# Update of x, squares and normalised tokens in two pieces of 512 columns at the stage boundaries of a four-layer network

## The chip, the cores and the metric

The kernel runs on one core of one Trainium2 chip. The metric is the device time of one launch in microseconds (us), median of the runs. The core has five engines with a queue each: PE (TensorE: matmuls and transposes; its weight loads are listed apart as PEld), DVE (VectorE), ACT (ScalarE), POOL (GpSimd) and SP (SyncE, which issues the loads of weights). An engine takes its queue in order; between engines, semaphores say when a result is there.

## The reference, cut to what matters

```python
def rms_norm(x, g):
    y = x * lax.rsqrt(jnp.mean(x * x, axis=-1, keepdims=True) + RMS_EPS)
    return y * g

def swiglu(x, w_gate, w_up, w_down):
    return (jax.nn.silu(x @ w_gate) * (x @ w_up)) @ w_down

for i in range(DEPTH):                                   # 4 layers
    f = swiglu(rms_norm(x, norm_pre[i, 0]), ...)
    x = x + FFN_HALF * rms_norm(f, norm_post[i, 0])      # FFN_HALF = 0.5
    hn = rms_norm(x, norm_pre[i, 1])
    m = dilated, differential or sliding-window attention of hn, by i % 3
    x = x + rms_norm(m, norm_post[i, 1])
    f = swiglu(rms_norm(x, norm_pre[i, 2]), ...)
    x = x + FFN_HALF * rms_norm(f, norm_post[i, 2])
```

x has 256 tokens of 1024 columns, the FFN 2816 inner columns; everything is fp32.

## The kernel before

**Stages.** Each layer is three stages, an FFN, a mixer (attention) and a second FFN, numbered s = 0 to 11 through the network; s = 1, 4, 7, 10 are the mixers. Between stage s and stage s + 1 lies a boundary; there are eleven. The 256 tokens are two token blocks, t = 0 and t = 1, of 128 tokens each, which lie on the 128 partitions; x stays on the chip as `x[:, t]`, 128 x 1024 for each t.

**Products.** An fp32 product is made of three matmuls of a cheaper type: `mm3` (L173 to L176) multiplies hi by hi, hi by lo and lo by hi, where hi is a rounded copy of an operand and lo what the rounding left off. So each weight unit (128 x 2048, 1 MB) is loaded by SP into a raw buffer (`load_next`, 3 raw buffers), then split (`split_next`): hi is a cast on ACT (L141), lo a subtraction on DVE or, for one unit at each boundary, on POOL (L142). Four units may be split ahead. `pump` takes up the units that are used and starts the next split and load for each.

**A boundary.** `closing` runs the last product of a stage, whose result (`acc`, two banks of 512 columns) is the f or m of the reference. Its last units (four in an FFN) are done for token block 0 first, then `boundary_elem(0)`; then for token block 1, and within the last of these units `norm_tr(0)` is placed; then `boundary_elem(1)`. For one token block, `boundary_elem_` does:

- ACT: Square of the two halves of acc, each with its row sum (L249).
- DVE: u = acc x factor x gain, in two halves (L255).
- POOL: `rstd_of`, the mean (L219) and its power -1/2 (L221).
- DVE: x = u x rstd + x, one instruction of 1024 columns (L259).
- then `norm_elem` for the next stage: ACT Square of x with row sum (L230), POOL mean (L217) and power (L221), DVE hn = x x rstd x gain (L235).

`norm_tr_` then brings hn into the layout of the next stage: PE transposes four blocks of 128 columns into a bank (L281), ACT casts the bank to the hi part of xT (L284), DVE subtracts to get the lo part (L285). This is done twice for each token block: the first L281, L284, L285 for columns 0 to 511, the second for columns 512 to 1023.

**The next stage's start.** An FFN starts with the products g (gate) of token block 0 with two units, then u (up) of token block 0 with two units, then the same for token block 1; `norm_tr(1)` stands in the middle of the last u unit of token block 0. A mixer starts in the same manner with `lead` products. The third matmul of an mm3, L176, takes xT's lo part, which L285 wrote; L174 and L175 take the hi part, which L284 wrote. In the mixer of s = 7 the lead products end with a bias product (L592), whose operand cb is written by ACT and DVE (L450).

**What sets the order.** The Tile framework's scheduler writes each engine's queue when the program is built, from the dependences, priorities (`boundary_elem` runs at a raised priority, PRI = 300; `norm_tr(0)` at PR2 = 8) and its own costs. So an edit may move instructions that it doesn't touch. At the last boundary (s = 11, the end of the program) x is updated in two pieces of 512 columns already (L265), since each is stored at once.

Of the kernel before, what the change touches and what calls it, by code (L numbers as in the profile page):

```python
# [8 lines left out]
F32 = mybir.dt.float32  # L9
F32R = mybir.dt.float32r  # L10
BF16 = mybir.dt.bfloat16
AF = mybir.ActivationFunctionType
ALU = mybir.AluOpType

P = 128
SEQ = 256
D = 1024
# [28 lines left out]
def tile_network(  # L46
# [27 lines left out]
    act, dve, pe, pool = nc.scalar, nc.vector, nc.tensor, nc.gpsimd  # L74
# [4 lines left out]
    small = ctx.enter_context(tc.tile_pool(name="small", bufs=6))  # L79
# [99 lines left out]
    x = actp.tile([P, 2, D], F32, name="x")  # L179
# [31 lines left out]
    def rstd_of(a, b, whole=False):  # L211

        ms = small.tile([P, 1], F32, tag="ms", name="ms")
        if whole:
            pool.tensor_scalar(out=ms, in0=a, scalar1=b, scalar2=None, op0=ALU.add)
        elif b is None:
            pool.tensor_scalar(out=ms, in0=a, scalar1=EPS, scalar2=None, op0=ALU.add)  # L217
        else:
            pool.tensor_scalar(out=ms, in0=a, scalar1=b, scalar2=EPS, op0=ALU.add, op1=ALU.add)  # L219
        r = small.tile([P, 1], F32, tag="rstd", name="rstd")  # L220
        state["rstd"] = pool.tensor_tensor(out=r, in0=ms, in1=half, op=ALU.pow).ins  # L221
        return r
# [2 lines left out]

    def norm_elem(t, s, parts=1):

        ss = small.tile([P, 1], F32, tag="ssx", name="ssx")
        hn = actp.tile([P, D], F32, tag="w", name="hn", bufs=3)
        act.activation(out=hn, in_=x[:, t], func=AF.Square, scale=1.0 / 32.0, accum_out=ss)  # L230
        r = rstd_of(ss, None)
        state["norm"] = state["rstd"]
        for c in range(parts):
            cs = slice(c * D // parts, (c + 1) * D // parts)
            i = dve.scalar_tensor_tensor(out=hn[:, cs], in0=x[:, t, cs], scalar=r, in1=gains["pre", s][:, cs],  # L235
                                     op0=ALU.mult, op1=ALU.mult)
        hn_of[t] = hn, s
        return i

    def boundary_elem(t, s, acc, mid):  # L240
        mid()
        with tc.high_priority(PRI):
            boundary_elem_(t, s, acc)

    def boundary_elem_(t, s, acc):

        ss = small.tile([P, 2], F32, tag="ssf", name="ssf")
        for i in range(2):
            act.activation(out=junk, in_=acc[i], func=AF.Square, scale=1.0 / 32.0,  # L249
                           accum_out=ss[:, i:i + 1])  # L250
        u = actp.tile([P, 2, 512], F32, tag="w", name="u", bufs=3)
        fac = 1.0 if s % 3 == 1 else 0.5
        g = gains["post", s].rearrange("p (i n) -> p i n", i=2)
        for i in range(2):
            dve.scalar_tensor_tensor(out=u[:, i], in0=acc[i], scalar=fac, in1=g[:, i],  # L255
                                     op0=ALU.mult, op1=ALU.mult)
        r = rstd_of(ss[:, 0:1], ss[:, 1:2])
        if s + 1 < 3 * DEPTH:
            dve.scalar_tensor_tensor(out=x[:, t], in0=u.rearrange("p i n -> p (i n)"), scalar=r,  # L259
                                     in1=x[:, t], op0=ALU.mult, op1=ALU.add)  # L260
            norm_elem(t, s + 1)
            return
        for i in range(2):
            cs = slice(i * 512, (i + 1) * 512)
            dve.scalar_tensor_tensor(out=x[:, t, cs], in0=u[:, i], scalar=r, in1=x[:, t, cs],  # L265
                                     op0=ALU.mult, op1=ALU.add)
            nc.sync.dma_start(out=out[:, t, cs], in_=x[:, t, cs])
# [739 lines left out]
    if True:  # L1007
# [10 lines left out]
        with tc.high_priority(PRI):  # L1018
            i = norm_elem(0, 0, 2)
            j = norm_tr(0)  # L1020
# [3 lines left out]
        with tc.issue_after(j.ins):  # L1024
            norm_elem(1, 0)
# [158 lines left out]
```

## Time and profile before

| | us |
|---|---|
| median of 3 runs | 2312.66 (2312.63 to 2313.06) |
| the profiled execution | 2313.26 |
| its span, first to last instruction | 2311.4 |

The mean granted clock of TensorE over the span is 0.998 of full speed. 32467 instructions ran. The core read 401.5 MB from memory, 174 GB/s over the span. Of the chain of work that ended last, 91% is PE's, 3% DVE's, and 2% each POOL's and ACT's.

The span is what the profiler saw of instructions; the profiled execution's own time is 1.9 us more. Busy times are sums over the span, a share of it stands behind each. A timeline row gives an instruction's start and duration, and in brackets how long the engine stood idle before it and which instruction's end released it, where that is known. Matmuls are pipelined, so one begins before its predecessor's end: their pace is read from the starts.

### The profile page before, as it was taken

The numbers are of one execution on the slowest core, as the hardware profiler recorded it, in microseconds if no ns is written. First come the engines' busy times: TensorE is split into PE (matmuls) and PEld (weight loads), VectorE is DVE, ScalarE is ACT, GpSimd is POOL, SyncE is SP. The second block draws the span as 40 slices with busy tenths as digits, with TensorE's granted clock in tenths as the row PEclk, the third lists the DMA queues.
The fourth block names the chain that finished last, engine by engine and source line by source line (L and its number), as shares of the span: only waits on it lengthen the run. The fifth ranks groups of instructions, "written<-read, shape, count | busy, mean of one in ns | idle before, by whom it ended". The sixth has DMA issues, their size and how long they took to land.

```text
span 2311.4 us, 32467 instructions
## 1 busy us (share of the span) xinstructions
PE 2278.0 (99%) x12912; PEld 1999.4 (87%) x12912; DVE 1252.8 (54%) x1830; ACT 1199.0 (52%) x2102; POOL 634.0 (27%) x640
## 2 busy tenths in 40 slices
PE   8999999999999999999999999999999999999998
PEld 6888999988888889788888887788888899998887
DVE  6545544565455555565465558655655544446553
ACT  5435666654444446654354448544444466666442
POOL 0004877620020028620020024100200287773000
PEclk9999999999999999999999999999999999999999
DMA  7554444445545544255555542555555544343552
GB/s 286 185 186 172 171 151 151 155 182 182 182 183 211 183 162 176 92 218 182 185 203 188 187 169 92 191 191 182 190 192 183 190 169 151 140 156 139 216 182 91
DMA packets 60498, 404.65 MB, mean 175 GB/s; under 512 B 6965, under 2 KB 7866, under 8 KB 16314
## 3 DMA queue, kind: packets, MB, share of 16 engines
q1 hardware_dynamic: 60202, 402.51, 47.9%
q8 instruction: 101, 1.65, 0.3%
q14 instruction: 51, 0.42, 0.1%
q10 hardware_dynamic: 144, 0.07, 0.0%
HBM read 401.50 MB, written 1.05 MB: 174 GB/s over the span
## 4 chain that ended last, share of the span: by engine, by line
PE 91%; DVE 3%; POOL 2%; ACT 2%; issue 1%; DMA 1%; SPq 0%; POOLq 0%; DVEq 0%; ACTq 0%
PE gu L175 11%; PE gu L176 11%; PE gu L174 11%; PE acc L176 8%; PE acc L174 8%; PE acc L175 7%; PE qk L175 4%; PE qk L174 4%; PE qk L176 4%; PE v L174 2%; PE v L175 2%; PE v L176 2%; PE tp L373 2%; PE tp L816 2%; POOL lo L142 1%; DVE lo L142 1%
## 5 line engine op out<-in xcount | busy, mean ns | idle before, releaser
L141 ACT CAST hi<-raw 128x1024 fp32r<-128x1024 f32 (+2 forms) x970 | 776.1, 845 | 765.5 <-PE gu L176 322.5
L142 DVE TENSOR_TENSOR lo<-raw,hi 128x1024 fp32r<-128x1024 f32 (+1 forms) x546 | 661.5, 1250 | 549.6 <-ACT hi L141 549.3
L142 POOL TENSOR_TENSOR lo<-raw,hi 128x512 fp32r<-128x512 f32 (+1 forms) x424 | 546.7, 1324 | 147.7 <-ACT hi L141 147.4
L174 PE MATMUL gu<-hi,xT 128*128 128x512 f32 (+1 forms) x1280 | 474.2, 370 | 0.0
L176 PE MATMUL gu<-hi,xT 128*128 128x512 f32 (+1 forms) x1280 | 471.0, 368 | 0.0
L175 PE MATMUL gu<-lo,xT 128*128 128x512 f32 (+1 forms) x1280 | 471.0, 368 | 0.0
L219 POOL TENSOR_SCALAR ms<-ssf 128x1 f32<-128x1 f32 x24 | 7.2, 302 | 1418.9 <-ACT junk L249 1417.9
L176 PE MATMUL acc<-hi,hT 128*128 128x512 f32 x704 | 276.1, 392 | 0.0
L175 PE MATMUL acc<-lo,hT 128*128 128x512 f32 x704 | 275.9, 392 | 0.0
L176 PEld LDWEIGHTS gu<-hi,xT 128*128 128x128 f32 x1280 | 241.3, 188 | 40.0
L174 PE MATMUL acc<-hi,hT 128*128 128x512 f32 x704 | 275.6, 391 | 0.0
L174 PEld LDWEIGHTS gu<-hi,xT 128*128 128x128 f32 x1280 | 241.4, 189 | 39.2
L175 PEld LDWEIGHTS gu<-lo,xT 128*128 128x128 f32 x1280 | 241.4, 189 | 39.1
L174 PE MATMUL qk<-xT,hi 128*128 128x256 f32 x800 | 225.7, 282 | 0.0
L175 PE MATMUL qk<-xT,hi 128*128 128x256 f32 x800 | 222.8, 279 | 0.0
L176 PE MATMUL qk<-xT,lo 128*128 128x256 f32 x800 | 222.7, 278 | 0.0
L176 PEld LDWEIGHTS acc<-hi,hT 128*128 128x128 f32 x704 | 132.2, 188 | 28.4
L175 PEld LDWEIGHTS acc<-lo,hT 128*128 128x128 f32 x704 | 132.2, 188 | 27.8
L174 PEld LDWEIGHTS acc<-hi,hT 128*128 128x128 f32 x704 | 132.3, 188 | 26.2
L174 PEld LDWEIGHTS qk<-xT,hi 128*128 128x128 f32 x800 | 151.3, 189 | 0.2
L176 PEld LDWEIGHTS qk<-xT,lo 128*128 128x128 f32 x800 | 150.6, 188 | 0.1
L175 PEld LDWEIGHTS qk<-xT,hi 128*128 128x128 f32 x800 | 150.3, 188 | 0.2
(265 smaller groups left out, 3364.6 us busy)
## 6 DMA issues: line engine op xcount, KB each, us to landing
raw<-in_w_ffn_dram SPq DMA_DIRECT2D x263, 1024.0 KB, 4.8
raw<-in_w_a_qk_dram SPq DMA_DIRECT2D x48, 1024.0 KB, 4.8
raw<-in_w_a_v_dram SPq DMA_DIRECT2D x32, 768.0 KB, 4.2
raw<-in_w_a_out_dram SPq DMA_DIRECT2D x8, 1024.0 KB, 4.8
raw<-in_w_b_qk_dram SPq DMA_DIRECT2D x8, 1024.0 KB, 4.8
gain<-in_g_pre_dram SPq DMA_DIRECT2D x12, 512.0 KB, 6.1
gain<-in_g_post_dram SPq DMA_DIRECT2D x12, 512.0 KB, 7.2
raw<-in_w_b_v_dram SPq DMA_DIRECT2D x4, 1024.0 KB, 4.8
```

What stands on the lines that cost most here:

```text
L141: act.copy(out=hi[:, cs], in_=r[:, cs])
L142: eng.tensor_tensor(out=lo[:, cs], in0=r[:, cs], in1=hi[:, cs].bitcast(F32), op=ALU.subtract)
L174: pe.matmul(o, lhsT=a[0], rhs=b[0], start=first, stop=False)
L175: pe.matmul(o, lhsT=a[0], rhs=b[1], start=False, stop=False)
L176: pe.matmul(o, lhsT=a[1], rhs=b[0], start=False, stop=last)
L219: pool.tensor_scalar(out=ms, in0=a, scalar1=b, scalar2=EPS, op0=ALU.add, op1=ALU.add)
L373: pe.transpose(tp[:, i * P:(i + 1) * P], h[:, i * P:(i + 1) * P], ident)
L816: pe.transpose(tp[:, c0:c0 + P], src, ident)
```

## The change

For the eleven boundaries, the update of x becomes two instructions of 512 columns, and `norm_elem` is called with two parts: its Square becomes two ACT instructions of 512 columns with a sum each, hn two DVE instructions of 512 columns, and POOL's mean adds the two sums. In the changed file lines stand lower by some: L230 is L232, L235 is L238, L249 is L252, L255 is L258, L259 is L264, L281 is L286, L284 is L289, L285 is L290; L141, L142, L174 to L176 and L217 to L221 stay. At the program's start, `norm_elem(0, 0, 2)` had hn in two parts already; there the Square becomes two as well.

```diff
--- before.py
+++ after.py
@@ -225,10 +225,13 @@
 
     def norm_elem(t, s, parts=1):
 
-        ss = small.tile([P, 1], F32, tag="ssx", name="ssx")
+        ss = small.tile([P, 2], F32, tag="ssx", name="ssx")
         hn = actp.tile([P, D], F32, tag="w", name="hn", bufs=3)
-        act.activation(out=hn, in_=x[:, t], func=AF.Square, scale=1.0 / 32.0, accum_out=ss)
-        r = rstd_of(ss, None)
+        for c in range(parts):
+            cs = slice(c * D // parts, (c + 1) * D // parts)
+            act.activation(out=hn[:, cs], in_=x[:, t, cs], func=AF.Square, scale=1.0 / 32.0,
+                           accum_out=ss[:, c:c + 1])
+        r = rstd_of(ss[:, 0:1], ss[:, 1:2] if parts == 2 else None)
         state["norm"] = state["rstd"]
         for c in range(parts):
             cs = slice(c * D // parts, (c + 1) * D // parts)
@@ -256,9 +259,11 @@
                                      op0=ALU.mult, op1=ALU.mult)
         r = rstd_of(ss[:, 0:1], ss[:, 1:2])
         if s + 1 < 3 * DEPTH:
-            dve.scalar_tensor_tensor(out=x[:, t], in0=u.rearrange("p i n -> p (i n)"), scalar=r,
-                                     in1=x[:, t], op0=ALU.mult, op1=ALU.add)
-            norm_elem(t, s + 1)
+            for i in range(2):
+                cs = slice(i * 512, (i + 1) * 512)
+                dve.scalar_tensor_tensor(out=x[:, t, cs], in0=u[:, i], scalar=r, in1=x[:, t, cs],
+                                         op0=ALU.mult, op1=ALU.add)
+            norm_elem(t, s + 1, 2)
             return
         for i in range(2):
             cs = slice(i * 512, (i + 1) * 512)
```

How instructions move, at the boundary from s = 2 to s = 3. In these rows an instruction is named by line, operation, output <- inputs and the output's size; x2 means two of them in a row.

**DVE, before**, from the first L285 of token block 0, by way of token block 1's u, to token block 1's hn:

```order
L285 TENSOR_TENSOR xT<-tp,xT 128x4x128
L142 TENSOR_TENSOR lo<-raw,hi 128x1024
L255 SCALAR_TENSOR_TENSOR u<-acc,gain 128x512 x2
L285 TENSOR_TENSOR xT<-tp,xT 128x4x128
L259 SCALAR_TENSOR_TENSOR x<-u,rstd,x 128x1024
L142 TENSOR_TENSOR lo<-raw,hi 128x1024 x2
L235 SCALAR_TENSOR_TENSOR hn<-x,rstd,gain 128x1024
```

DVE, now, the same stretch:

```order
L290 TENSOR_TENSOR xT<-tp,xT 128x4x128
L142 TENSOR_TENSOR lo<-raw,hi 128x1024
L258 SCALAR_TENSOR_TENSOR u<-acc,gain 128x512 x2
L264 SCALAR_TENSOR_TENSOR x<-u,rstd,x 128x512 x2
L290 TENSOR_TENSOR xT<-tp,xT 128x4x128
L142 TENSOR_TENSOR lo<-raw,hi 128x1024
L238 SCALAR_TENSOR_TENSOR hn<-x,rstd,gain 128x512 x2
L142 TENSOR_TENSOR lo<-raw,hi 128x1024
```

The second subtraction for token block 0 (L285, now L290) stood ahead of token block 1's update of x and now stands behind it; one split moved behind hn. The first of these holds at all eleven boundaries.

**PE, before**, in the start of the FFN s = 3, token block 0 (hi and lo are the weights' parts); the last three rows are the first matmuls that read the second half of xT:

```order
L176 MATMUL g<-hi,xT 128x512
L174 MATMUL g<-hi,xT 128x512
L175 MATMUL g<-lo,xT 128x512
L176 MATMUL g<-hi,xT 128x512
L174 MATMUL g<-hi,xT 128x512
L175 MATMUL g<-lo,xT 128x512
L176 MATMUL g<-hi,xT 128x512
```

PE, now, from the same L174 that was fifth above:

```order
L174 MATMUL g<-hi,xT 128x512
L175 MATMUL g<-lo,xT 128x512
L174 MATMUL u<-hi,xT 128x512
L175 MATMUL u<-lo,xT 128x512
L176 MATMUL u<-hi,xT 128x512
L174 MATMUL u<-hi,xT 128x512
L176 MATMUL g<-hi,xT 128x512
```

Four u matmuls, which read the first half of xT, moved ahead of the first L176 of g that reads the second half's lo part. In the starts of mixers eleven lead matmuls of 256 columns moved ahead in the same way.

**ACT, before**, at token block 0's boundary from s = 2 to s = 3, from its first Squares to its first cast of xT:

```order
L249 ACTIVATE junk,ssf<-acc 128x512 x2
L141 CAST hi<-raw 128x1024
L230 ACTIVATE hn,ssx<-x 128x1024
L141 CAST hi<-raw 128x1024
L141 CAST hi<-raw 128x512 x4
L141 CAST hi<-raw 128x1024
L284 CAST xT<-tp 128x4x128
```

ACT, now:

```order
L252 ACTIVATE junk,ssf<-acc 128x512 x2
L232 ACTIVATE hn,ssx<-x 128x512
L141 CAST hi<-raw 128x1024
L232 ACTIVATE hn,ssx<-x 128x512
L141 CAST hi<-raw 128x1024
L141 CAST hi<-raw 128x512 x4
L141 CAST hi<-raw 128x1024
L289 CAST xT<-tp 128x4x128
```

The first half of the Square moved ahead of a split cast, the second half kept its place behind it. So it is at the seven boundaries that end an FFN; at the four that end a mixer the halves stand side by side. POOL's order is as before.

## Rows read from the trace of the kernel before

**Rows 1.** Page, part 1: busy us (share of the span) x instructions.

```profile
PE 2278.0 (99%) x12912; PEld 1999.4 (87%) x12912; DVE 1252.8 (54%) x1830; ACT 1199.0 (52%) x2102; POOL 634.0 (27%) x640
```

**Rows 2.** Waits of PE's weight loads, whole span: us in total, times, longest us.

```profile
PEld g L176 <- DVE xT L285: 7.6, 13, 1.5
...
PEld lead L176 <- DVE xT L285: 3.5, 7, 0.9
```

**Rows 3.** Timeline, DVE, s = 2 to 3: start us, us, instruction.

```profile
672.10 1.28 DVE L255 SCALAR_TENSOR_TENSOR u<-acc,gain 128x512 f32<-128x512 f32 x2
673.30 0.68 DVE L285 TENSOR_TENSOR xT<-tp,xT 128x512 fp32r<-128x512 f32 x1
674.42 1.29 DVE L259 SCALAR_TENSOR_TENSOR x<-u,rstd,x 128x1024 f32<-128x1024 f32 x1 [0.45 <-POOL rstd L221]
```

**Rows 4.** Timeline, PE, s = 2 to 3.

```profile
673.04 0.39 PE L174 MATMUL g<-hi,xT 128*128 128x512 f32 x1
673.27 0.39 PE L175 MATMUL g<-lo,xT 128*128 128x512 f32 x1
674.03 0.50 PE L176 MATMUL g<-hi,xT 128*128 128x512 f32 x1 [0.37 <-DVE xT L285]
```

**Rows 5.** Timeline, POOL, s = 2 to 3.

```profile
673.83 0.56 POOL L221 TENSOR_TENSOR rstd<-ms,half 128x1 f32<-128x1 f32 x1
```

**Rows 6.** Timeline, DVE, end of the program (s = 11).

```profile
2306.46 1.41 DVE L265 SCALAR_TENSOR_TENSOR x<-u,rstd,x 128x512 f32<-128x512 f32 x2 [0.34 <-POOL rstd L221]
```

**Rows 7.** Timeline, ACT, DVE, PE, s = 2 to 3, token block 0.

```profile
662.09 1.05 ACT L230 ACTIVATE hn<-x 128x1024 f32<-128x1024 f32 x1
...
664.21 1.28 DVE L235 SCALAR_TENSOR_TENSOR hn<-x,rstd,gain 128x1024 f32<-128x1024 f32 x1 [0.77 <-POOL rstd L221]
...
665.92 0.27 PE L281 MATMUL tp<-ident,hn 128*128 128x128 f32 x1
```

**Rows 8.** Timeline, PE and DVE, first and last of six FFN starts.

```profile
486.13 0.50 PE L176 MATMUL g<-hi,xT 128*128 128x512 f32 x1
...
486.52 1.28 DVE L259 SCALAR_TENSOR_TENSOR x<-u,rstd,x 128x1024 f32<-128x1024 f32 x1 [0.45 <-POOL rstd L221]
...
2121.49 0.50 PE L176 MATMUL g<-hi,xT 128*128 128x512 f32 x1
...
2121.89 1.29 DVE L259 SCALAR_TENSOR_TENSOR x<-u,rstd,x 128x1024 f32<-128x1024 f32 x1 [0.45 <-POOL rstd L221]
```

**Rows 9.** Timeline, DVE and PE, s = 7 to 8.

```profile
1463.74 0.68 DVE L285 TENSOR_TENSOR xT<-tp,xT 128x512 fp32r<-128x512 f32 x1
...
1464.48 0.50 PE L176 MATMUL g<-hi,xT 128*128 128x512 f32 x1
```

**Rows 10.** Timeline, POOL, PE, DVE, mixer starts (s = 0, 3, 6).

```profile
203.70 0.56 POOL L221 TENSOR_TENSOR rstd<-ms,half 128x1 f32<-128x1 f32 x1
...
204.61 0.45 PE L176 MATMUL lead<-hi,xT 128*128 128x384 f32 x1 [0.46 <-DVE xT L285]
...
861.94 0.38 PE L176 MATMUL lead<-hi,xT 128*128 128x256 f32 x1 [0.68 <-DVE xT L285]
...
863.87 0.28 PE L174 MATMUL lead<-hi,xT 128*128 128x256 f32 x1
863.91 1.28 DVE L259 SCALAR_TENSOR_TENSOR x<-u,rstd,x 128x1024 f32<-128x1024 f32 x1 [2.02 <-POOL rstd L221]
863.98 0.28 PE L175 MATMUL lead<-lo,xT 128*128 128x256 f32 x1
...
869.65 0.52 PE L281 MATMUL tp<-ident,hn 128*128 128x128 f32 x3 [0.52 <-DVE hn L235]
...
1369.61 0.38 PE L174 MATMUL lead<-hi,xT 128*128 128x256 f32 x1 [0.67 <-DVE u L255]
...
1371.96 1.28 DVE L259 SCALAR_TENSOR_TENSOR x<-u,rstd,x 128x1024 f32<-128x1024 f32 x1 [1.80 <-POOL rstd L221]
...
1378.14 0.36 PE L592 MATMUL lead<-cb,ones 128*128 128x256 f32 x1 [1.66 <-DVE cb L450]
```

## The prediction

> **What bounds the kernel now.** I read the page's busy shares first: TensorE (PE) is busy 99% of the span, VectorE (DVE) 54%, ScalarE (ACT) 52% [rows 1]. A change to DVE and ACT work can therefore move the time only where PE waits for them. The table of waits, for PE's weight loads, shows how much that is at the boundaries: loads of the g and lead matmuls waited 7.6 and 3.5 us for xT, the low parts of the transposed normalised tokens that L285 writes on DVE [rows 2]. That is 11.1 us of 2311.4.
>
> One boundary, s = 2 to s = 3, shows how such a wait arises. On DVE the second L285 of token block 0 runs from 673.30 to 673.98, and then the update of x for token block 1 (L259) from 674.42 [rows 3]. On PE the matmuls of g are issued 0.23 us apart (673.04, 673.27); the next, L176, is the first to read that second half of xT's low part and starts at 674.03, 0.05 after L285's end, having idled 0.37 [rows 4]. On POOL, rstd of token block 1 ends at 673.83 + 0.56 = 674.39 [rows 5], and L259 starts 0.03 later: it waits for POOL, L285 does not.
>
> **What is moved.** Two L285 of token block 0 remain two, but the scheduler now puts the two pieces of token block 1's update ahead of the second one, as the DVE rows of the order show; it does so at all eleven boundaries. DVE takes its queue in order, so L285, which needs only transposes that ended long before, now stands behind an instruction that waits for POOL's rstd. Behind L285 waits PE. That is the step on which I rest the forecast; the halves themselves are a side matter.
>
> **The price of a boundary.** Two 512-column pieces from SBUF take 1.41 us end to end [rows 6], where L259 took 1.29 [rows 3]. The next instruction starts 0.08 before its predecessor ends (L255's pair ends at 673.38, L285 starts at 673.30) [rows 3]. So from the start of the update to PE's L176: 1.41 - 0.08, then L285's 0.68, then 0.05, in all 2.06 us.
>
> *Starts of an FFN, six of seven.* At s = 2: 674.42 + 2.06 = 676.48 instead of 674.03, 2.45 us later. The scheduler fills part of it: four u matmuls now stand ahead of the waiting L176 (the PE rows of the order), 4 x 0.23 = 0.92 us of work that is no longer to be done after it. Net 1.53. The first such start gives 486.52 + 2.06 - 486.13 = 2.45, the last 2121.89 + 2.06 - 2121.49 = 2.46 [rows 8]; the three between are alike. Six times 1.53: **9.2 us**. Bounds of one: 0.41 if rstd were ready when u is done (673.30 + 2.06 - 674.03 - 0.92), 2.45 if the four matmuls fill nothing. I take the value between, since both rows that make it are of this very place.
>
> *The seventh, s = 7 to 8.* Here rstd is early and the update already follows L285 without a gap: 1463.74 + 2.06 = 1465.80 for PE's 1464.48 [rows 9], 1.32 later, less 0.92: **0.4 us**.
>
> *Starts of a mixer.* There eleven 256-column matmuls move ahead of the wait, at 0.11 us each (863.87, 863.98) [rows 10], 1.2 us. At s = 0, rstd ends at 203.70 + 0.56, the pieces start at 204.29, PE's L176 at 206.35 instead of 204.61: 1.74 - 1.2 = 0.5; s = 9 has the same pattern. Together **1.0 us**. At s = 3 rstd is late: L259 started only at 863.91, after 2.02 us of waiting for POOL, while PE had gone on at 861.94 [rows 10]: 863.91 + 2.06 - 861.94 = 4.03, less 1.2, is 2.8; the transposes at 869.65 idled 0.52 for hn, which comes at about the old time, so that idling goes: **2.3 us**. At s = 6 L259 started at 1371.96, so L176 can start at 1374.02; PE went on at 1369.61 [rows 10] and has sixteen matmuls to do before it, to about 1371.4: 2.6 us of new waiting. Of that, 1.66 us stood before L592 at 1378.14 anyway, waiting for cb: **0.9 us** (0.9 to 2.6, because cb's DVE instruction now has one more split ahead of it).
>
> **What I cost at nothing.** Token block 0's chain: the ACT rows of the order show its second Square behind the split cast L141, so halves give no head start where that cast stands; the old Square also ran after that cast, at 662.09 [rows 7]. hn ended at 664.21 + 1.28 = 665.49 and PE's transposes have a fixed place at 665.92 [rows 7]: 0.43 us of cover. If it were gone, PE would wait by what the chain is late, some 0.2 us a boundary. Halving hn lets the first transposes begin earlier, but PE does not ask earlier. The 44 added DVE and 23 added ACT instructions lie in engines that are half idle. Token block 1's hn ends about where it did, because its squares in halves follow the update closely; its transposes stand far behind in PE's order, and PE is later by then. One split (L142) now comes after hn of token block 1, so its SP load of the next weights also starts later; three raw and four split buffers cover that. POOL's order of instructions is unchanged but for the form of the mean. At the program's start, L230 becomes two halves before the first transposes, but PE's first matmul waits there for a cast behind the weight casts.
>
> **Sum.** 9.2 + 0.4 + 1.0 + 2.3 + 0.9 = 13.8 us more. The profiled execution took 2313.26, so 2327.1; that execution stands 0.6 above the median of the runs, 2312.66, so the forecast for the median is **2326.5 us**, 0.6% slower.
>
> **A rule for the other side.** The rows say that DVE and ACT are half idle and that PE waits for them all the same [rows 1, 2]. The Trainium skill, page "Perfetto Trace Analysis", section "Optimizing Scalar/DVE Operations", says of just that case that breaking up instructions may let work be completed sooner. By it the change would win; no run here shows it yet, and the second rival gives its time from rows.
>
> **Rivals.**
> *Small loss, 2315.6.* Only if token block 1's rstd came earlier than now, by the 0.44 us and more for which L259 waits, would the pieces cost their 1.33 us and no wait: 0.41 at each of seven FFN starts, near nothing at mixers, some 3 us. Against it: POOL's instructions ahead of rstd are the same as before. Chance 0.10.
> *Faster, 2301.6.* The mechanism: the halves let squares and updates overlap, xT is complete when PE asks, and the 11.1 us of [rows 2] go. It decides if L285 is early enough, that is before 673.3 at s = 2, as DVE comes to it sooner. For it speaks that hn's first half is ready 0.7 us earlier. Against it: L285 stands behind the update in DVE's order, which starts at 674.4. Chance 0.05.
> *Worse, up to 2338.8.* The moved matmuls fill nothing, because they wait for something themselves: 6 x 2.45 + 1.32 + 2 x 1.74 + 4.03 + 2.6 = 26.1 us. Against it: the weights that they read are split before L285 in DVE's order. Chance 0.04.
> That the change does not do what it says is excluded by the order of the built programs.
>
> **How the numbers follow.** The forecast has the remaining 0.81. Its own spread comes from the terms with wide bounds: one boundary of the six 0.4 us off either way gives 2.4 us, s = 3 and s = 6 another 2 to 3 us. The range 2318 to 2332 holds this case nearly whole and leaves out the rivals, 0.19. A measurement of this kernel tells about 0.2% from no change, 4.6 us: the forecast and the worse rival are slower, the small loss counts as the same, so 0.05 faster, 0.10 same, 0.85 slower.
>
> **What would show it.** Right: PE's waits of g and lead for xT grow from 11.1 us to some 25, L285's second start of each boundary stands directly behind the second piece of the update, and the update still starts within 0.05 us of rstd's end. At s = 3 PE's one wait is 3 us or more. Wrong: L285 before the update, or PE's L176 within 0.5 us of its old place in the boundary, or a wait for u's weights ahead of it. Wrong in size if rstd of token block 1 moves by more than 0.5 us.

## The result, and the profile after

The changed kernel takes 2328.04 us (median of 4 runs, 2326.39 to 2330.08), the kernel before 2312.64 in the same comparison (4 runs, 2312.24 to 2313.06): a ratio of 1.0065, with a 95% interval of 1.0052 to 1.0077. It is slower by some 15.4 us. The profiled execution of the changed kernel took 2328.22 us with a span of 2326.4, so its trace is 15.0 us longer than the trace before.

The busy times of the page answer to [rows 1]; columns are as there.

```profile
PE 2279.2 (98%) x12912; PEld 2000.2 (86%) x12912; DVE 1264.5 (54%) x1874; ACT 1202.7 (52%) x2148; POOL 635.1 (27%) x640
```

Hardly any work was added: PE is busy 1.2 us more, DVE 11.7. So nearly all of the 15 us are time in which PE waits. The table of waits of PE's weight loads answers to [rows 2] (us in total, times, longest):

```profile
PEld g L176 <- DVE xT L290: 18.6, 13, 2.4
PEld lead L176 <- DVE xT L290: 9.1, 8, 2.1
```

The waits for the lo part of xT went from 11.1 us to 27.7. At s = 2 to 3, DVE's timeline shows the moved subtraction behind the second piece of the update, where the order of the program had it; [rows 3] has it ahead.

```profile
676.01 1.28 DVE L258 SCALAR_TENSOR_TENSOR u<-acc,gain 128x512 f32<-128x512 f32 x2
677.21 1.40 DVE L264 SCALAR_TENSOR_TENSOR x<-u,rstd,x 128x512 f32<-128x512 f32 x2
678.53 0.68 DVE L290 TENSOR_TENSOR xT<-tp,xT 128x512 fp32r<-128x512 f32 x1
```

The pieces take 1.40 us end to end, and L290 starts 0.08 before they end. Both had been taken from [rows 3, 6]. PE at the same place answers to [rows 4]:

```profile
672.48 0.39 PE L175 MATMUL g<-lo,xT 128*128 128x512 f32 x1
674.53 0.50 PE L176 MATMUL g<-hi,xT 128*128 128x512 f32 x1 [1.66 <-DVE xT L290]
...
679.27 0.50 PE L176 MATMUL g<-hi,xT 128*128 128x512 f32 x1 [0.81 <-DVE xT L290]
```

Here is what I had not foreseen: PE waits twice. The wait at 679.27 is that for the moved subtraction. The wait at 674.53, the longer one, is for the first half's lo part. In the kernel before, that was written just in time:

```profile
669.87 0.68 DVE L285 TENSOR_TENSOR xT<-tp,xT 128x512 fp32r<-128x512 f32 x1
...
670.61 0.50 PE L176 MATMUL g<-hi,xT 128*128 128x512 f32 x1
```

L285 ended at 670.55, and PE took L176 0.32 us after L175 (670.29), where its pace is 0.23. So this path had nothing to spare. The wait comes from token block 0's chain, which I had costed at nothing. Three timelines of token block 0 at s = 2 to 3 show how, against [rows 7]; ACT's first:

```profile
663.20 0.63 ACT L232 ACTIVATE hn<-x 128x512 f32<-128x512 f32 x1 [1.86 <-DVE x L264]
663.83 1.04 ACT L141 CAST hi<-raw 128x1024 fp32r<-128x1024 f32 x1
664.77 0.63 ACT L232 ACTIVATE hn<-x 128x512 f32<-128x512 f32 x1
```

POOL's:

```profile
667.03 3.52 POOL L142 TENSOR_TENSOR lo<-raw,hi 128x512 fp32r<-128x512 f32 x2
```

DVE's, with PE's first transpose in its place in time:

```profile
666.95 2.45 DVE L238 SCALAR_TENSOR_TENSOR hn<-x,rstd,gain 128x512 f32<-128x512 f32 x2 [0.82 <-POOL rstd L221]
...
668.10 0.27 PE L286 MATMUL tp<-ident,hn 128*128 128x128 f32 x1
...
669.33 2.31 DVE L142 TENSOR_TENSOR lo<-raw,hi 128x1024 fp32r<-128x1024 f32 x1
671.56 2.31 DVE L142 TENSOR_TENSOR lo<-raw,hi 128x1024 fp32r<-128x1024 f32 x1
673.79 0.68 DVE L290 TENSOR_TENSOR xT<-tp,xT 128x512 fp32r<-128x512 f32 x1
```

The two halves of hn taken apart (shortest, median and longest in ns, then the first and the last start in us):

```profile
L238 DVE SCALAR_TENSOR_TENSOR hn<-x,rstd,gain x2: 753/1266/1780, 667.0 to 667.6; 128x512 f32<-128x512 f32 x2
```

The second half of the Square starts 1.57 us after the first, because a split cast of 1.04 us stands between them. hn starts 1.15 us ahead of PE's first transpose, where in [rows 7] it started 1.71 ahead: 0.56 us later. Then its two halves take 2.45 us in all (0.75 the first, 1.78 the second), where the update's two pieces take 1.40. Between the starts of these halves, at 667.03, POOL begins its own split (L142). PE's transposes keep their place, as I had said; but behind hn stand two splits in DVE's queue, and then L290 at 673.79, with PE waiting. From hn's start to that L290 it is 6.84 us, where it was 5.66 (664.21 to 669.87): 1.18 more, and hn itself takes 1.17 more (2.45 for 1.28). With the 0.56 that makes 1.74, and PE takes its L176 2.05 us after L175 instead of 0.32, which is 1.73 later.

A second surprise stands at s = 4 to 5. After a wait of 1.94 us, PE's matmuls are at first issued 0.23 us apart and then 0.43:

```profile
1002.22 0.50 PE L176 MATMUL g<-hi,xT 128*128 128x512 f32 x1 [1.94 <-DVE xT L290]
1002.56 0.40 PE L174 MATMUL g<-hi,xT 128*128 128x512 f32 x1
1002.80 0.39 PE L175 MATMUL g<-lo,xT 128*128 128x512 f32 x1
...
1003.66 0.63 PE L175 MATMUL g<-lo,xT 128*128 128x512 f32 x1
1004.09 0.63 PE L176 MATMUL g<-hi,xT 128*128 128x512 f32 x1
```

The table by stretches shows TensorE's granted clock (the column before DMA's share; the columns ahead of it are each engine's busy time and instructions):

```profile
1002.20:1003.60 1.40, 1.38 (x5) 1.17 (x6) 1.10 (x1) 1.38 (x3) 1.09 (x2) 0.88 1.10 456
1003.60:1006.60 3.00, 3.00 (x8) 2.31 (x7) 2.48 (x3) 0.59 (x2) 0.49 (x1) 0.50 0.96 401
```

The clock fell from full speed, 2.4 GHz, to half, 1.2 GHz, for about 3 us, soon after that wait. Eight matmuls at 0.43 instead of 0.23 cost some 1.6 us there. Every trace here has one such fall amid the mixer s = 4 (at 962 us in the kernel before); this one is new.

### The profile page after: what moved, and what is told of

It is laid out like the page before. It is cut to its first block, busy times and chain, and to the rows that moved or that the text cites. A ratio compares the mean times of both kernels' runs of the same rounds, so it can differ in the third digit from the quotient of the medians.

```text
span 2326.4 us, 32581 instructions
## 1 busy us (share of the span) xinstructions
PE 2279.2 (98%) x12912; PEld 2000.2 (86%) x12912; DVE 1264.5 (54%) x1874; ACT 1202.7 (52%) x2148; POOL 635.1 (27%) x640
## 3 DMA queue, kind: packets, MB, share of 16 engines
q8 instruction: 101, 1.65, 0.3%
## 4 chain that ended last, share of the span: by engine, by line
PE 87%; POOL 5%; DVE 3%; ACT 2%; issue 2%; DMA 0%; SPq 0%; POOLq 0%; DVEq 0%; ACTq 0%
PE gu L176 11%; PE gu L175 11%; PE gu L174 11%; PE acc L174 7%; PE acc L176 7%; PE acc L175 7%; POOL lo L142 4%; PE qk L174 4%; PE qk L175 4%; PE qk L176 4%; PE v L174 2%; PE v L175 2%; PE v L176 2%; PE tp L378 2%; PE tp L821 2%
## 5 line engine op out<-in xcount | busy, mean ns | idle before, releaser
L141 ACT CAST hi<-raw 128x1024 fp32r<-128x1024 f32 (+2 forms) x970 | 774.9, 844 | 761.0 <-PE gu L176 323.5
L142 DVE TENSOR_TENSOR lo<-raw,hi 128x1024 fp32r<-128x1024 f32 (+1 forms) x546 | 661.7, 1250 | 549.2 <-ACT hi L141 549.1
L142 POOL TENSOR_TENSOR lo<-raw,hi 128x512 fp32r<-128x512 f32 (+1 forms) x424 | 543.0, 1313 | 147.6 <-ACT hi L141 146.8
L174 PE MATMUL gu<-hi,xT 128*128 128x512 f32 (+1 forms) x1280 | 474.2, 370 | 0.0
L176 PE MATMUL gu<-hi,xT 128*128 128x512 f32 (+1 forms) x1280 | 471.0, 368 | 0.0
L175 PE MATMUL gu<-lo,xT 128*128 128x512 f32 (+1 forms) x1280 | 471.0, 368 | 0.0
L176 PE MATMUL acc<-hi,hT 128*128 128x512 f32 x704 | 276.1, 392 | 0.0
L175 PE MATMUL acc<-lo,hT 128*128 128x512 f32 x704 | 275.9, 392 | 0.0
L176 PEld LDWEIGHTS gu<-hi,xT 128*128 128x128 f32 x1280 | 241.2, 188 | 40.0
L174 PE MATMUL acc<-hi,hT 128*128 128x512 f32 x704 | 275.6, 391 | 0.0
L175 PEld LDWEIGHTS gu<-lo,xT 128*128 128x128 f32 x1280 | 241.4, 189 | 39.1
L174 PEld LDWEIGHTS gu<-hi,xT 128*128 128x128 f32 x1280 | 241.3, 189 | 39.2
L174 PE MATMUL qk<-xT,hi 128*128 128x256 f32 x800 | 225.7, 282 | 0.0
L175 PE MATMUL qk<-xT,hi 128*128 128x256 f32 x800 | 222.7, 278 | 0.0
L176 PE MATMUL qk<-xT,lo 128*128 128x256 f32 x800 | 222.7, 278 | 0.0
L176 PEld LDWEIGHTS acc<-hi,hT 128*128 128x128 f32 x704 | 132.1, 188 | 28.4
L175 PEld LDWEIGHTS acc<-lo,hT 128*128 128x128 f32 x704 | 132.2, 188 | 28.0
L174 PEld LDWEIGHTS acc<-hi,hT 128*128 128x128 f32 x704 | 132.3, 188 | 26.1
L174 PEld LDWEIGHTS qk<-xT,hi 128*128 128x128 f32 x800 | 151.3, 189 | 0.2
L176 PEld LDWEIGHTS qk<-xT,lo 128*128 128x128 f32 x800 | 150.5, 188 | 0.1
L175 PEld LDWEIGHTS qk<-xT,hi 128*128 128x128 f32 x800 | 150.4, 188 | 0.2
```

The costliest lines, as they stand in the source:

```text
L141: act.copy(out=hi[:, cs], in_=r[:, cs])
L142: eng.tensor_tensor(out=lo[:, cs], in0=r[:, cs], in1=hi[:, cs].bitcast(F32), op=ALU.subtract)
L174: pe.matmul(o, lhsT=a[0], rhs=b[0], start=first, stop=False)
L175: pe.matmul(o, lhsT=a[0], rhs=b[1], start=False, stop=False)
L176: pe.matmul(o, lhsT=a[1], rhs=b[0], start=False, stop=last)
```

## The experiments

The diffs of the first six are against the changed kernel or, where it is said, another run; those of the last four against the kernel before. To see where time goes I compared each trace with that of the kernel before: both issue 12912 PE instructions, and the order differs mostly near the boundaries, so in the middle of each stage the same-numbered instruction can be compared, and the growth of the difference from one stage's middle to the next is put down to the boundary between. The table stands behind the first four.

**The update alone in pieces.** Square and hn whole, against the changed kernel:

```diff
-            norm_elem(t, s + 1, 2)
+            norm_elem(t, s + 1)
```

> Only the update of x in two pieces; Square and hn whole as before. On DVE the second subtraction of token block 0 (L290's work) still stands behind token block 1's two update pieces at all eleven boundaries; ACT's order is as in the kernel before. Theory A (that place in DVE's queue makes PE wait): nearly the whole loss stays, 2324 to 2329 us; at s = 2 to 3 PE's first L176 of g does not wait (under 0.1 us), the second one waits 2 to 2.5 us. Rival B (the halves of Square and hn make token block 0's xT late, since POOL's split gets in between the halves of hn and holds it up): 2312 to 2315 us. If both count and overlap, about as A.

Measured: 2332.32 us (4 runs, 2331.06 to 2333.61), ratio 1.0082 (1.0068 to 1.0096), 3 us above what theory A had allowed and slower than the whole change. DVE and PE, at s = 2 and at s = 5:

```profile
675.56 1.41 DVE L264 SCALAR_TENSOR_TENSOR x<-u,rstd,x 128x512 f32<-128x512 f32 x2 [1.03 <-POOL rstd L221]
676.89 0.68 DVE L290 TENSOR_TENSOR xT<-tp,xT 128x512 fp32r<-128x512 f32 x1
```

```profile
677.63 0.50 PE L176 MATMUL g<-hi,xT 128*128 128x512 f32 x1 [1.96 <-DVE xT L290]
...
1194.77 0.50 PE L176 MATMUL g<-hi,xT 128*128 128x512 f32 x1 [1.95 <-DVE xT L290]
```

There is one wait at each of these boundaries, for the moved subtraction, and none for token block 0's first half: A's place is right. The table by stretches has what is above A's range, behind the wait at s = 2 and behind the equal one at s = 5:

```profile
679.10:682.10 3.00, 3.00 (x15) 2.46 (x14) 2.42 (x2) 0.60 (x1) 0.33 (x1) 1.00 1.02 425
...
1196.20:1199.20 3.00, 3.00 (x9) 2.35 (x8) 2.42 (x2) 0.60 (x1) 0.36 (x1) 0.51 0.97 407
```

After the wait of 1.96 us the clock stayed at full speed, after that of 1.95 it went to half for 3 us. So it went at five places of this trace where the trace before has no fall, at 1.5 to 1.6 us each (the starts of the matmuls there against those at full clock), some 7.8 us in all. Without them the trace would be some 12.5 us longer than before, if no other wait had taken their place.

**Square and hn alone in pieces.** The update whole.

```diff
-            for i in range(2):
-                cs = slice(i * 512, (i + 1) * 512)
-                dve.scalar_tensor_tensor(out=x[:, t, cs], in0=u[:, i], scalar=r, in1=x[:, t, cs],
-                                         op0=ALU.mult, op1=ALU.add)
+            dve.scalar_tensor_tensor(out=x[:, t], in0=u.rearrange("p i n -> p (i n)"), scalar=r,
+                                     in1=x[:, t], op0=ALU.mult, op1=ALU.add)
             norm_elem(t, s + 1, 2)
```

> Only Square and hn in two pieces; the update whole. On DVE the second subtraction of token block 0 stands ahead of token block 1's update, as before. Theory A (order on DVE): 2312 to 2314 us, no change. Rival B (hn's second half is held up by POOL's split at boundaries that end an FFN): the second half of hn of token block 0 takes 1.5 to 1.9 us instead of 0.75, PE's first L176 of g at s = 2, 5 and 8 waits 1 to 1.8 us, in all 2317 to 2322 us.

Measured: 2319.5 us (8 runs, 2318.78 to 2319.64), ratio 1.0025 (1.0015 to 1.0036). POOL, DVE and PE at s = 2 to 3:

```profile
664.75 5.36 POOL L142 TENSOR_TENSOR lo<-raw,hi 128x512 fp32r<-128x512 f32 x3 [0.52 <-ACT hi L141]
...
664.26 2.45 DVE L238 SCALAR_TENSOR_TENSOR hn<-x,rstd,gain 128x512 f32<-128x512 f32 x2 [1.03 <-POOL rstd L221]
...
671.84 0.50 PE L176 MATMUL g<-hi,xT 128*128 128x512 f32 x1 [1.37 <-DVE xT L288]
```

As B had it: the halves take 2.45 us, POOL's split having begun at 664.75 between their starts, and PE's first L176 waits 1.37. The order on DVE was that of before, so this loss is of another kind.

**The change with the order kept.**

```diff
-                dve.scalar_tensor_tensor(out=x[:, t, cs], ...)
+                with tc.issue_after(state["xlo"]) if t else ExitStack():
+                    dve.scalar_tensor_tensor(out=x[:, t, cs], ...)
```

(`state["xlo"]` is token block 0's last subtraction of `norm_tr_`; `issue_after` orders the queue and adds no wait.)

> The whole change, but token block 1's update pieces are queued on DVE behind the second subtraction of token block 0, as they were before. Theory A: the waits of PE's second L176 go, 2312 to 2315 us. Rival B: at s = 1 and 10, where a mixer ended and only the second L176 waited, the loss (1.4 us each) goes, but at s = 2, 5 and 8 the first L176 waits its 1.8 us still; in all 2318 to 2322 us. If neither is right, 2327 to 2329.

Measured: 2321.45 us (5 runs, 2319.88 to 2321.69), ratio 1.0033 (1.0021 to 1.0046). PE and DVE at s = 2 to 3:

```profile
673.26 0.50 PE L176 MATMUL g<-hi,xT 128*128 128x512 f32 x1 [1.66 <-DVE xT L291]
...
675.94 0.68 DVE L291 TENSOR_TENSOR xT<-tp,xT 128x512 fp32r<-128x512 f32 x1
676.54 1.40 DVE L265 SCALAR_TENSOR_TENSOR x<-u,rstd,x 128x512 f32<-128x512 f32 x2
...
676.67 0.50 PE L176 MATMUL g<-hi,xT 128*128 128x512 f32 x1 [0.40 <-DVE xT L291]
```

The subtraction is back ahead of the update and PE's second L176 waits 0.40 us, about as in [rows 4]; the first still waits 1.66, and at s = 1 and 10 the loss is gone: rival B had this and the time. Of the 15.0 us, 6.5 went by the order (15.0 less 8.5 of this trace). This trace has two falls of the clock of its own, at s = 3 and 6, each behind a wait of 1.88 us, and not the change's fall at s = 4, so 6.5 is a round figure.

**The change with Square whole.** One Square of 1024 columns, hn and update in pieces.

```diff
-        for c in range(parts):
-            cs = slice(c * D // parts, (c + 1) * D // parts)
-            act.activation(out=hn[:, cs], in_=x[:, t, cs], ..., accum_out=ss[:, c:c + 1])
-        r = rstd_of(ss[:, 0:1], ss[:, 1:2] if parts == 2 else None)
+        act.activation(out=hn, in_=x[:, t], ..., accum_out=ss[:, 0:1])
+        r = rstd_of(ss[:, 0:1], None)
```

> The change with the Square of x whole, update and hn in pieces; order on DVE as in the change, order on ACT as before. Theory C (a split cast stands between the halves of Square, so rstd comes 0.6 us later, and that makes token block 0's xT late): PE's first L176 at s = 2, 5 and 8 waits no longer; the second waits 2 to 2.5 us; in all 2325 to 2328 us. Theory B (POOL gets in between the halves of hn): the second half of hn still takes over 1.5 us and the first L176 still waits over 0.5 us; 2326 to 2329 us. The waits tell them apart, not the time.

Measured: 2325.24 us (5 runs, 2324.64 to 2326.79), ratio 1.0052 (1.0038 to 1.0066). DVE and PE:

```profile
665.40 2.45 DVE L235 SCALAR_TENSOR_TENSOR hn<-x,rstd,gain 128x512 f32<-128x512 f32 x2 [0.76 <-POOL rstd L221]
...
672.99 0.50 PE L176 MATMUL g<-hi,xT 128*128 128x512 f32 x1 [1.11 <-DVE xT L287]
```

The halves of hn still take 2.45 us, and PE's first L176 still waits 1.11 of its 1.66. So most of that wait is hn's, and the split Square adds the other 0.55: both B and C have a part, C's claim that the wait goes is wrong, and the time lies in C's range alone.

The cost of each boundary against the kernel before, in us, worked out from the traces as said above (s is the stage that ends; s = 4 and s = 7 take in the end of their mixers, where the change has -0.9 and +0.5 that are not the boundary's):

| s | forecast | change | update only | order kept | norm only | POOL held back |
|---|---|---|---|---|---|---|
| 0 | 0.5 | 0.51 | 0.26 | 0.71 | 0.15 | 1.26 |
| 1 | 1.53 | 1.44 | 1.54 | -0.09 | 0.24 | 0.24 |
| 2 | 1.53 | 2.13 | 1.55 | 1.73 | 1.43 | 0.08 |
| 3 | 2.3 | 1.68 | 3.54 | 1.65 | 0.77 | 0.49 |
| 4 | 1.53 | 2.57 | 3.79 | 0.29 | 1.35 | -0.78 |
| 5 | 1.53 | 2.13 | 3.17 | 1.74 | 1.45 | 0.05 |
| 6 | 0.9 | -0.04 | 1.76 | -0.01 | -0.61 | 1.61 |
| 7 | 0.4 | 0.28 | 0.63 | -0.19 | 0.33 | 0.62 |
| 8 | 1.53 | 2.13 | 3.17 | 1.75 | 1.41 | 0.07 |
| 9 | 0.5 | 0.51 | 0.08 | 0.71 | 0.16 | 1.27 |
| 10 | 1.53 | 1.43 | 1.55 | -0.11 | 0.23 | 0.24 |
| before s = 0 and at the end | 0 | 0.22 | -0.70 | 0.28 | -0.59 | -0.32 |
| whole span | 13.8 | 14.99 | 20.34 | 8.46 | 6.32 | 4.83 |

**POOL held back.** Against the run with Square and hn alone in pieces: POOL's first split piece is made to wait for the second half of hn.

```diff
+                if c == 0 and i in on_pool and "hn_last" in state:
+                    tc.add_manual_dep(z.ins, state["hn_last"].name, mybir.DependencyInfo(
+                        mybir.DependencyClass.Sync, mybir.DependencyReason.DATA), reason="pool after hn")
```

> The run with Square and hn in pieces and the update whole, with one wait more: POOL's first split at a boundary starts only when the second half of token block 0's hn is done. Theory B: the second half of hn takes 0.75 us instead of 1.5 to 1.8, PE's first L176 at s = 2, 5 and 8 waits under 0.5 us instead of 1.53, and the time goes back to 2312 to 2315 us. Rival: if the hn halves are late for the later rstd and not for POOL, the wait stays over 1 us and the time at 2318 to 2320; if POOL's split is itself in need, its later start makes a new wait and 2316 or more.

Measured: 2318.07 us (11 runs, 2316.39 to 2320.6), ratio 1.0022 (1.0013 to 1.0031). DVE and POOL at s = 2 to 3:

```profile
665.68 1.41 DVE L241 SCALAR_TENSOR_TENSOR hn<-x,rstd,gain 128x512 f32<-128x512 f32 x2 [1.04 <-POOL rstd L224]
...
667.23 2.16 POOL L142 TENSOR_TENSOR lo<-raw,hi 128x512 fp32r<-128x512 f32 x1 [1.58 <-ACT hi L141]
```

The two halves now take 1.41 us, and at s = 2, 5 and 8 nothing is left of the 1.4 us (last column of the table). That bears out B's mechanism: the same two instructions, with the same operands, took 2.45 with POOL's split begun between them and 1.41 without. (The first split behind hn also took 1.22 us here and 2.31 in the change, so more than hn's own 1.04 us came free; the next run, with hn whole, leaves POOL as it was. At s = 0, 7 and 9 a piece of POOL's still ran beside the halves in spite of the edge, and there the second one still took 1.5 to 1.8 us.) The Trainium skill, page "SBUF — State Buffer", section "SBUF: two separate sides", says that DVE, for an operation with two inputs from SBUF, and GpSimd, for one that reads SBUF, share a port pair that whichever starts first holds for its whole instruction. The rows here agree: the second half takes 1.78 us where POOL begins before it and some 0.75 where POOL is held back, and hn whole takes 1.28 (next run) though POOL's split begins while it runs. But the time came back only in part. At s = 0 and 9 PE waits 1.5 us for token block 1's hn, since POOL's rstd of token block 1 now comes late behind its delayed splits. At s = 6 PE waits 2.78 us for cb, where [rows 10] has 1.66, and a fall of the clock follows. The waits speak against the first rival of the expectation, though its time holds the measured one; the second was right.

**The order kept, with hn whole.** Against the run with the order kept; Square and update stay in pieces.

```diff
-        for c in range(parts):
-            cs = slice(c * D // parts, (c + 1) * D // parts)
+        for c in range(1 if s else parts):
+            cs = slice(0, D) if s else slice(c * D // parts, (c + 1) * D // parts)
             i = dve.scalar_tensor_tensor(out=hn[:, cs], ...)
```

> The run with the order kept, with hn whole again: update and Square in two pieces, token block 1's update behind the second subtraction of token block 0. Theory B (POOL's split takes its turn between the two halves of hn and holds the second one up): hn of token block 0 at s = 2 to 3 takes 1.28 us in one piece as before, and of the 1.82 us that PE's first L176 waited with the order kept, the 1.27 that stayed with a whole Square go; 0.3 to 0.7 us stay from the later rstd. In all 2313 to 2316 us. Theory C (the split Square alone makes the wait): 1.8 us stay, 2320 to 2322.

Measured: 2320.16 us (6 runs, 2319.85 to 2320.96), ratio 1.0032 (1.0019 to 1.0044). DVE, POOL and PE at s = 2 to 3, and PE at s = 0 to 1:

```profile
665.37 1.28 DVE L238 SCALAR_TENSOR_TENSOR hn<-x,rstd,gain 128x1024 f32<-128x1024 f32 x1 [0.82 <-ACT hi L141]
...
665.45 4.58 POOL L142 TENSOR_TENSOR lo<-raw,hi 128x512 fp32r<-128x512 f32 x2
...
671.76 0.50 PE L176 MATMUL g<-hi,xT 128*128 128x512 f32 x1 [0.21 <-DVE xT L291]
...
211.16 0.41 PE L287 MATMUL tp<-ident,hn 128*128 128x128 f32 x2 [2.03 <-DVE hn L238]
```

At s = 2 to 3 B's numbers hold: hn takes 1.28 us, PE's first L176 waits 0.21 instead of 1.66. The whole time missed B's range all the same, by what it costs at the starts of mixers. The last row shows one place: PE waits 2.03 us for token block 1's hn, and s = 0 and 9 cost 1.4 and 1.5 us. Now POOL is the one that is held up (its first two pieces take 4.58 us, against 3.52 in the change), and rstd of token block 1 stands behind them in POOL's queue. So in the change DVE's queue hands the delay on, here POOL's. The largest part, 3.6 us, stands at s = 6: PE waits 2.19 us for cb, a fall of the clock follows, and further on in the mixer it waits 2.91 us for DVE's sp (L812), where the same matmul waited 0.48 us in the kernel before. What makes these two late is open.

**No pieces at all, only the order.** The kernel before, with the second subtraction queued behind token block 1's update of 1024 columns.

```diff
+            if t:
+                tc.add_manual_dep(state["xlo"], z.ins.name, mybir.DependencyInfo(
+                    mybir.DependencyClass.NoSync, mybir.DependencyReason.DATA), reason="behind x")
```

> The kernel before with no instruction split: one edge in DVE's queue puts the second subtraction of token block 0 behind token block 1's update of 1024 columns, as it stands in the change behind the pieces (the scheduler also puts one split ahead of that update). Theory A (the place in the queue is the cost, the pieces are not): PE's second L176 at s = 2, 5 and 8 waits 2.0 to 2.6 us, and where a wait passes 2.1 us PE may come back at half clock for some 3 us, as in the run with the update alone in pieces; 2328 to 2335 us. Rival (the pieces themselves cost): 2312 to 2315 us.

Measured: 2322.54 us (5 runs, 2321.77 to 2322.7), ratio 1.0037 (1.0025 to 1.005). DVE, PE and POOL at s = 2 to 3:

```profile
676.55 1.28 DVE L259 SCALAR_TENSOR_TENSOR x<-u,rstd,x 128x1024 f32<-128x1024 f32 x1 [0.45 <-POOL rstd L221]
677.75 0.68 DVE L288 TENSOR_TENSOR xT<-tp,xT 128x512 fp32r<-128x512 f32 x1
...
678.49 0.50 PE L176 MATMUL g<-hi,xT 128*128 128x512 f32 x1 [1.56 <-DVE xT L288]
...
675.07 1.44 POOL L221 TENSOR_TENSOR rstd<-ms,half 128x1 f32<-128x1 f32 x1
```

No instruction is split, and it is slower by some 9 us: an order of the queue costs without any pieces. Not all of it is the subtraction's place: the split that went ahead of the update runs on DVE while POOL makes rstd, and rstd's power takes 1.44 us instead of the 0.56 of [rows 5], so the update starts 0.9 us later. Both ranges missed. A's was too high: the scheduler here moved nine u matmuls ahead of the waiting L176 (four in the change), which with the later update leaves a wait of 1.56 us, and the clock fell behind none of the boundaries' waits, not even that of 2.22 us at s = 3. So the 2.1 us of the expectation is borne out by no run; in the run with the update alone a wait of 1.95 had a fall behind it.

**The subtraction earlier than before.** The kernel before, whole instructions, with token block 1's u behind that subtraction.

```diff
+            with tc.issue_after(state["xlo"]) if t and s < 11 and s != 6 else ExitStack():
                 dve.scalar_tensor_tensor(out=u[:, i], in0=acc[i], scalar=fac, in1=g[:, i],
```

> The kernel before, whole instructions throughout, with one edge in DVE's queue: u of token block 1 behind the second subtraction of token block 0 (not at s = 6, where the next stage waits for u). Theory A read the other way: if the place of that subtraction is what PE waits for, an earlier place takes away the half microsecond of wait at s = 2, 4, 5, 8 and 0, 9 and 0.84 at s = 3, some 4 us: 2307 to 2311 us. Rival: the scheduler now also puts a split ahead of token block 1's update, so that hn of token block 1 comes some 0.8 us later and its transposes wait: 2311 to 2316.

Measured: 2308.33 us (11 runs, 2307.55 to 2309.53), ratio 0.9979 (0.997 to 0.9988): 4.7 us faster than the kernel before, and than the change by 20. DVE and PE at s = 2 to 3:

```profile
670.73 0.68 DVE L286 TENSOR_TENSOR xT<-tp,xT 128x512 fp32r<-128x512 f32 x1
671.33 1.27 DVE L256 SCALAR_TENSOR_TENSOR u<-acc,gain 128x512 f32<-128x512 f32 x2
...
671.86 0.39 PE L175 MATMUL g<-lo,xT 128*128 128x512 f32 x1
672.08 0.39 PE L176 MATMUL g<-hi,xT 128*128 128x512 f32 x1
```

The subtraction (670.73) now stands ahead of u, PE issues L176 0.22 us after L175, and the wait of [rows 4] is gone. What the rival named happens at s = 0 and 9 alone, where PE's transposes wait 0.78 us for hn. The trace is 5.7 us shorter than before; 1.2 of that lies ahead of the first boundary, where the edge does nothing.

**The same with the update in pieces, and the same with the update ahead of the split.**

```diff
 (update in pieces, beside the edge)
+            for i in range(2):
+                dve.scalar_tensor_tensor(out=x[:, t, cs], ...)
 (update ahead of the split: boundary_elem)
-        mid()
         with tc.high_priority(PRI):
             boundary_elem_(t, s, acc)
+        with tc.issue_after(state["xu"]) if s < 11 else ExitStack():
+            mid()
```

> The same edge with the update of x in two pieces (Square and hn whole); here the pieces follow u directly and the two splits stand behind them. If only places in queues count and the pieces cost no more than 0.1 us each: as the run with whole instructions or up to 2 us below it, 2306 to 2311 us. If the pieces themselves cost time: 2313 or more.

> The kernel before with the second subtraction of token block 0 ahead of token block 1's u (not at s = 6), and the split that the scheduler then put ahead of token block 1's update queued behind it. Theory A: as the run with the edge alone (2308.3 us), less the 0.8 us each at s = 0 and 9 that the transposes of token block 1 waited for hn there: 2306 to 2308 us. If these waits come from POOL's chain and not from that split: 2308 to 2309.

Measured: 2314.08 us (11 runs, 2312.1 to 2314.99), ratio 1.0004 (0.9995 to 1.0012), with the pieces; 2311.0 (11 runs, 2310.2 to 2312.07), ratio 0.9989 (0.998 to 0.9998), whole with the update ahead. Both missed what was expected: in both, two splits now stand between the update and token block 1's hn, and PE waits for that hn at its transposes (at s = 2, 0.32 us with pieces, 0.17 whole). More is lost at s = 3, 4 and 6; in both traces the clock falls at s = 6. Between these two DVE's order is the same but for s = 4 and 6, so their boundaries at s = 2, 5 and 8 compare the pieces alone: they cost 0.12 to 0.13 us more each, which is 1.41 less 1.29. Most of the 3 us between the two runs is not this: 1.3 of it stand at s = 4 and 6, where the order differs.

## Why the prediction was right, point by point

**The time and the direction** were right: 15.4 us of loss against 13.8 forecast. The step on which the forecast rested was right too: the subtraction that PE waits for was moved behind an update that waits for other work. The run with no pieces at all shows that an order of this kind costs 9 us by itself (with one split moved as well), and the run with the order kept that undoing it gives 6.5 back. How near the sum came is in part luck, as follows.

**The price of a boundary** (2.06 us from the start of the update to PE's L176) measured 679.27 - 677.21 = 2.06. **The fill** by the moved matmuls was right where nothing else is wrong: 1.53 forecast, 1.44 and 1.43 measured at s = 1 and 10, and 1.54 to 1.55 at s = 1, 2 and 10 of the run with the update alone.

**The step that failed** is the one headed as costing nothing: "0.43 us of cover. If it were gone, PE would wait by what the chain is late, some 0.2 us a boundary." I followed token block 0's hn to PE's transposes, which did keep their place. I did not follow it down DVE's own queue, where two splits and the first subtraction stand behind it with nothing to spare, nor did I ask what the split Square and the split hn open to others: a cast between the halves of Square (hn starts 0.56 us later at s = 2) and POOL's split between the halves of hn (1.17 us more than hn whole; 1.04 of it is POOL's, 2.45 less 1.41). PE's first L176 then waits 1.66 us at s = 2, and as much at s = 5 and 8.

**Why the sum held all the same.** The two losses cover each other. Where PE has waited 1.66 us for the first half, it asks for the second that much later, and finds a wait of 0.81 instead of 1.96. Alone they cost 20.3 us (some 12.5 without the falls of the clock) and 6.3 to 8.5; together 15.0. At s = 2, 5 and 8 that leaves 2.13 for my 1.53, and s = 4 gave 1.0 more than forecast, with a fall of the clock (1.6 us) that I had not in the sum: the six FFN starts cost 11.8 for my 9.2. The starts of mixers made up for it: s = 3 and 6 cost 1.6 together for my 3.2. At s = 6 I had a wait of 2.6 us for the second half, less the old wait before the bias product [rows 10]; there was no such wait. PE waited 1.88 us for the first half instead, and the old wait went for it (1.8 us before, 0.2 after, in the table of waits). That the misses cancel, to 1.2 us, is luck.

**The 11.1 us of [rows 2]** I read as time that could be won or lost. They are waits of weight loads, which are issued ahead of their matmuls: at s = 2 the load waited 0.80 us, PE itself 0.37 [rows 4]. PE's own waits for these lo parts were 4.6 us in the kernel before:

```profile
PE g L176 <- DVE xT L285: 2.7, 5, 1.1
...
PE lead L176 <- DVE xT L285: 1.9, 5, 0.7
```

So the faster rival, which took off all 11.1 us, was priced too high; the run with the subtraction earlier, which leaves 2.0 of these 4.6, gained 4.7.

**"At s = 3 PE's one wait is 3 us or more"** fell: there are two, of 1.88 and 1.28. "The update still starts within 0.05 us of rstd's end" fell at s = 2 too: there it starts at 677.21, directly behind u, which token block 0's late splits had held up, and rstd had ended at 676.90.

**The rule of the Trainium skill** ("Perfetto Trace Analysis", "Optimizing Scalar/DVE Operations") was not borne out here: DVE and ACT were half idle (54% and 52% busy), PE waited for them, and breaking the instructions up made the waits of its weight loads longer (27.7 us for 11.1), by their places in the queues and by what got in between the halves.

**Open** is when the clock falls. In the run with the update alone, waits of 1.95 and 1.96 us on the same matmuls ended one with and one without a fall, and waits of 1.88 us at s = 3 and 6 had a fall behind them with the order kept and none in the change. The spread of the change's runs, 3.7 us against 0.8 before, could come from this; only one execution of it was traced.

## What to carry to other kernels

Before costing the halves of a split instruction, print the queues: what was moved ahead of what, on the engine that takes its instructions in order, can cost more than the halves give. Ask of each gap that the split opens which other instruction, of the same engine or of one that shares its port, will take it, and follow the queue behind the late piece to whoever waits on it. If a wait names a subtraction that has been ready for long, moving that one instruction forward is the cheaper change: here 4.7 us for one edge.

## What the runs showed of the hardware that I had not expected

Two DVE instructions of 512 columns with both inputs in SBUF took 2.45 us together when POOL's elementwise instruction began between them, and 1.41 when it was held back. After some of PE's waits (1.94 us in the change, 1.95 in the run with the update alone) its granted clock went to half for some 3 us, which cost 1.5 to 1.6 us each time; in the run with the update alone that was some 7.8 us, over a third of its loss. So one long wait can cost more than two shorter ones: the whole change, with two waits at s = 5, lost 2.13 us there, and the update alone, with one and a fall of the clock behind it, 3.17. At s = 2, where no fall followed, the one wait cost 1.55.
